# Moving the fourth weight sum's products later in three kinds of pair, its adding transfer into halves, one weight sum's transfer sooner, and one turned panel's reads to GpSimd's queue, in a two-layer encoder kernel

## The chip, the cores and the metric

The kernel runs on one core of a Trainium2 chip. The metric is device time in microseconds (us), the median of several runs. The profile is that of one execution on that core.

## The reference, cut to what matters

There are 256 tokens of width 2048, and two layers. Both layers end in the same kind of MLP, with a hidden width of 8192, and all matrices are float32:

```python
def sq_relu_mlp(h, g, w1, w2):
    a = jax.nn.relu(rms_norm(h, g) @ w1)
    return (a * a) @ w2
# layer 1:  proj = rms_norm(h) @ a_w_in -> q, k, v, forget gates
#           h = h + forgetting_attention(...) @ a_w_out
#           h = h + sq_relu_mlp(h, mlp_norm_g[0], mlp_w1[0], mlp_w2[0])
# shared:   kv = rms_norm(h) @ kv_w
# layer 2:  q = rms_norm(h) @ b_w_q ; chunked attention against kv
#           h = h + o @ b_w_out
#           h = h + sq_relu_mlp(h, mlp_norm_g[1], mlp_w1[1], mlp_w2[1])
```

The two MLPs are about 1270 us of the profiled span. The change touches them and the step ahead of each, the output projection of the attention.

## The kernel before, in words

**A unit of weights.** Weights come in units of 128 partitions x 1024 float32. ScalarE (ACT in the profile) rounds a unit to `hi` (line 323), and VectorE (DVE) makes `lo = raw - hi` (line 324). TensorE (PE) then multiplies in three passes: `hi` with the activations' `hi` (line 592), `hi` with the activations' `lo` (594), and `lo` with the activations' `hi` (596). So the second pass is the first that needs the activations' `lo`, and the third the first that needs the weights' `lo`. There are three buffers of `hi` and three of `lo`. A split can be issued when the unit three places earlier has been through its second pass.

**Pairs.** Two neighbouring panels of 512 output columns form a pair. For one half of the rows of a pair's weight matrix, the 2 x 2 blocks of tokens and columns go through seven products in place of eight, in the manner of Strassen and Winograd. The seven operands, or forms, are in this order 11, T3, T2, T1, 21, T4 and 22. The four T's are sums of weights:

- T3 = 22 + 12 and T2 = T3 + 11 are made by VectorE (`make`, line 964).
- T1 = 12 + 11 and T4 = T2 + 21 are made by a transfer that adds (`put`, line 974): GpSimd's queue sends the second operand from memory into the tile of the first.

Each form of the pairs here is two units (halves 0 and 1, six matmuls each). The other half of the rows goes the ordinary way, as units a4 to a7 (first panel) and b4 to b7 (second panel), of twelve matmuls each. b5, b6 and b7 of a pair are mixed into the start of the next pair.

**The order of pairs.** The hidden width is cut into four chunks c of 2048. W1(c,r) is the pair of the first matrix that gives hidden panels n = 2r and 2r+1 of chunk c, and W2(c,r) is the pair of the second matrix that uses chunk c. They run as W1(0,0), W1(0,1), then for each c: W2(c,0), W1(c+1,0), W2(c,1), W1(c+1,1). In the tables of the code W1(0,1) is called "second", W1(c,0) and W1(c,1) "ahead0" and "ahead1", and W2(c,0) and W2(c,1) "deep0" and "deep1".

**What sets the order.** `TABLES["ORD"]` gives for each kind of pair how the last three forms (F, named by `FO`) stand among the ordinary units. `run` goes through the units, and each time `fetch` sees to it that three splits are issued ahead. After each ordinary unit, and after each second half of a form, one call of `run_fill` issues one slot of side work. VectorE, ScalarE, TensorE and SyncE (SP, which issues most loads) keep the written order; GpSimd's order is the scheduler's.

**Side work.** A finished hidden panel is turned by 32 x 32 blocks (VectorE, line 440, tile z), crosses partitions by sixteen small transfers, half from SP's queue and half from GpSimd's (`hop`, line 466, into tile q), and then goes through `take`: relu in q (ACT line 1037), its square as `act` hi (ACT line 1042), the square in q (ACT line 1044), and `act` lo = q - hi (DVE line 1048). `TABLES["T"][n]` says, for chunks 1 to 3, in which slot after the panel's end each of these steps is issued. Panel 3 of chunk c ends with b7 of W1(c,1), inside W2(c,0), and the first unit that reads it is a6 of W2(c,0).

**Loads.** A pair's six numbers, such as `W2S`, say how many ordinary units before its start blocks 12, 22, 21 and 11 are loaded (SP's queue) and T3 and T1 are made, in this order. A load waits until the tile's old content has been split.

**The panel ahead of the MLP.** Each of the four finished panels of the residual stream is turned in the same way but through memory: one write, then four reads, both from SP's queue (`carry`, lines 450 and 456).

## Time and profile before

| what | value |
|---|---|
| device time, median of 3 runs | 2055.9 us (2054.76 to 2056.26) |
| span of the profiled execution, first to last instruction | 2051.8 us (no time of its own is given beside the span) |
| instructions | 27095 |
| PE busy | 2042.6 us, 9062 matmuls |
| DVE busy / ACT busy / POOL busy | 1784.1 / 1404.8 / 244.2 us |
| DMA | 557.78 MB, mean 272 GB/s |
| granted TensorE clock | 1.000 |

The span leaves 4.1 us of the median to what lies before the first and behind the last instruction. A busy PE is not by itself a PE at its peak, since matmuls overlap; whether it loses time is read from the starts of its matmuls and from its waits.

### The profile page before, as it was taken

The numbers are of one execution on the slowest core, as the hardware profiler recorded it, in microseconds if no ns is written. First come the engines' busy times: TensorE is split into PE (matmuls) and PEld (weight loads), VectorE is DVE, ScalarE is ACT, GpSimd is POOL, SyncE is SP. The second block draws the span as 40 slices with busy tenths as digits, with TensorE's granted clock in tenths as the row PEclk, the third lists the DMA queues.
The fourth block names the chain that finished last, engine by engine and source line by source line (L and its number), as shares of the span: only waits on it lengthen the run. The fifth ranks groups of instructions, "written<-read, shape, count | busy, mean of one in ns | idle before, by whom it ended". The sixth has DMA issues, their size and how long they took to land.

```text
span 2051.8 us, 27095 instructions
## 1 busy us (share of the span) xinstructions
PE 2042.6 (100%) x9062; PEld 1688.9 (82%) x9062; DVE 1784.1 (87%) x2065; ACT 1404.8 (68%) x1805; POOL 244.2 (12%) x351
## 2 busy tenths in 40 slices
PE   9999999999999999999999999999999999999999
PEld 8888888878888888888878888888888888888887
DVE  7788798899898898899988788889988988988996
ACT  7766676677677676677778666667866676776764
POOL 1121010021111102101012111100111111111020
PEclk9999999999999999999999999999999999999999
DMA  8898888898888898898879888888988888988985
GB/s 321 259 293 273 272 279 245 306 268 266 296 258 285 259 297 271 248 292 273 264 242 300 278 256 285 258 264 286 286 290 267 271 262 289 264 287 261 295 260 149
DMA packets 175021, 557.78 MB, mean 272 GB/s; under 512 B 40592, under 2 KB 69152, under 8 KB 152096
## 3 DMA queue, kind: packets, MB, share of 16 engines
q1 hardware_dynamic: 153824, 464.99, 63.7%
q0 software_dynamic: 20768, 90.75, 22.5%
q8 instruction: 71, 1.16, 0.2%
q14 instruction: 70, 0.57, 0.1%
q10 hardware_dynamic: 288, 0.30, 0.1%
HBM read 516.07 MB, written 27.29 MB: 265 GB/s over the span
## 4 chain that ended last, share of the span: by engine, by line
PE 94%; DVE 3%; DMA 1%; ACT 1%; issue 1%; SPq 0%; ACTq 0%; POOL 0%; DVEq 0%; POOLq 0%
PE acc L596 22%; PE acc L592 22%; PE acc L594 22%; PE s L596 9%; PE s L592 9%; PE s L594 9%; DVE lo L324 1%; DMA raw<-in_w_in 1%; PE po L729 1%; PE po L766 1%; ACT hi L323 0%; PE po L767 0%; PE po L728 0%; DMA turn<-z 0%; DMA raw<-in_w_qb 0%
## 5 line engine op out<-in xcount | busy, mean ns | idle before, releaser
L324 DVE TENSOR_TENSOR lo<-raw,hi 128x1024 fp32r<-128x1024 f32 (+1 forms) x409 | 494.1, 1212 | 80.4 <-ACT hi L323 76.3
L323 ACT ACTIVATE hi<-raw 128x1024 fp32r<-128x1024 f32 (+1 forms) x409 | 429.7, 1054 | 192.2 <-PE acc L594 131.0
L592 PE MATMUL acc<-hi,act 128*128 128x512 f32 x1774 | 496.2, 392 | 1.2 <-ACT hi L323 1.1
L596 PE MATMUL acc<-lo,act 128*128 128x512 f32 x1774 | 491.1, 390 | 1.5 <-DVE lo L324 1.4
L594 PE MATMUL acc<-hi,act 128*128 128x512 f32 x1774 | 490.3, 389 | 0.0
L596 PEld LDWEIGHTS acc<-lo,act 128*128 128x128 f32 x1774 | 332.3, 188 | 73.2 <-DVE lo L324 4.2
L594 PEld LDWEIGHTS acc<-hi,act 128*128 128x128 f32 x1774 | 332.9, 188 | 69.7
L592 PEld LDWEIGHTS acc<-hi,act 128*128 128x128 f32 x1774 | 331.4, 188 | 69.8 <-ACT hi L323 1.9
L323 ACT ACTIVATE hi<-w 128x1024 fp32r<-128x1024 f32 x254 | 267.1, 1058 | 127.9 <-PE acc L594 85.2
L324 DVE TENSOR_TENSOR lo<-wT,hi 128x1024 fp32r<-128x1024 f32 x220 | 267.1, 1221 | 65.0 <-ACT hi L323 61.4
L324 DVE TENSOR_TENSOR lo<-w,hi 128x1024 fp32r<-128x1024 f32 x254 | 305.5, 1218 | 15.3 <-ACT hi L323 13.5
L323 ACT ACTIVATE hi<-wT 128x1024 fp32r<-128x1024 f32 x220 | 232.0, 1060 | 97.3 <-PE acc L594 46.2
L592 PE MATMUL s<-hi,act 128*128 128x512 f32 x530 | 146.3, 391 | 0.2 <-ACT hi L323 0.2
L596 PE MATMUL s<-lo,act 128*128 128x512 f32 x530 | 145.2, 389 | 0.4 <-DVE lo L324 0.3
L594 PE MATMUL s<-hi,act 128*128 128x512 f32 x530 | 144.8, 388 | 0.0
L466 POOL DMA_DIRECT2D q<-z x192 | 95.6, 511 | 251.8 <-DVE z L440 217.3
L596 PEld LDWEIGHTS s<-lo,act 128*128 128x128 f32 x530 | 99.0, 188 | 22.0 <-DVE lo L324 1.7
L594 PEld LDWEIGHTS s<-hi,act 128*128 128x128 f32 x530 | 99.3, 188 | 20.7
L592 PEld LDWEIGHTS s<-hi,act 128*128 128x128 f32 x530 | 98.9, 188 | 20.9 <-ACT hi L323 0.8
L596 PE MATMUL s<-lo,S 128*128 128x512 f32 x288 | 88.8, 389 | 0.7 <-DVE lo L324 0.7
L592 PE MATMUL s<-hi,S 128*128 128x512 f32 x288 | 89.4, 392 | 0.0
L594 PE MATMUL s<-hi,S 128*128 128x512 f32 x288 | 88.7, 389 | 0.0
(217 smaller groups left out, 2285.6 us busy)
## 6 DMA issues: line engine op xcount, KB each, us to landing
raw<-in_w_in SPq DMA_DIRECT2D x75, 512.0 KB, 5.8
w<-in_w2fa SPq DMA_DIRECT2D x32, 1024.0 KB, 6.5
w<-in_w2fb SPq DMA_DIRECT2D x32, 1024.0 KB, 6.0
w<-in_w1fa SPq DMA_DIRECT2D x28, 1024.0 KB, 6.9
w<-in_w1fb SPq DMA_DIRECT2D x28, 1024.0 KB, 7.6
raw<-in_w2sa SPq DMA_DIRECT2D x52, 512.0 KB, 7.4
raw<-in_w2sb SPq DMA_DIRECT2D x50, 512.0 KB, 6.8
raw<-in_w_kv SPq DMA_DIRECT2D x48, 512.0 KB, 5.1
```

The costliest lines, as they stand in the source:

```text
L323: S.activation(hi[:, c], raw[:, c], AF.Copy)
L324: V.tensor_tensor(lo[:, c], raw[:, c], hi[:, c].bitcast(F32), op=ALU.subtract)
L466: (G if i % 2 else SY).dma_start(dst[32 * j : 32 * j + 32, i * n : (i + 1) * n], z[32 * i : 32 * i + 32, j * n : (j + 1) * n])
L592: TE.matmul(ps[:, cols], xh, cut(hi, j), start=first, stop=False, **kw)
L594: TE.matmul(ps[:, cols], xl, cut(hi, j), start=False, stop=False, **kw)
L596: TE.matmul(ps[:, cols], xh, cut(lo, j), start=False, stop=last, **kw)
L729: TE.matmul(s[:, P : 3 * P], q[:, a, P:T], k[:, a], start=True, stop=True)
L766: TE.matmul(po[:, :T], v[:, 0, a * P : (a + 1) * P], pT[:, :2], start=True, stop=False)
```

## The change

It has five parts.

1. In the pairs W2(c,0) with c of 1 to 3 (new kind "later0") T4 moves behind b4; in W1(c,0) and W1(c,1) with c of 1 to 3, T4 moves behind a5. The products are the same.
2. In all pairs of this kind (`deep`) the transfer that adds 21 into T2 is issued in two halves, each as soon as its half of T2 has been split. Before, only W1(0,1) did so.
3. In the pairs W2(c,1) the transfer that makes T1 is issued two ordinary units before the pair's start, not one.
4. For hidden panel 3 of chunks 1 to 3, the four steps of `take` are issued in slots 5, 6, 6, 6 after the panel's end, not in 4, 5, 5, 5.
5. The four reads of the last turned residual panel ahead of each MLP go to GpSimd's queue.

```diff
-    "FO": {..., "deep1": "456", "deep0": "465"},
+    "FO": {..., "deep1": "456", "deep0": "465", "later0": "465"},
-    "ORD": {..., "ahead1": "a4 F F a5 a6 a7 F b4", "ahead0": "F a4 F a5 a6 a7 F b4", ...
+    "ORD": {..., "ahead1": "a4 F a5 F a6 a7 F b4", "ahead0": "F a4 a5 F a6 a7 F b4", ...
         "deep0": "a4 F F F b4 a5 a6 a7",
+        "later0": "a4 F F b4 F a5 a6 a7"},
-    "T": (..., (0, -1, 4, 5, 5, 5)),
+    "T": (..., (0, -1, 5, 6, 6, 6)),
-    "W2L": (6, 5, 5, 5, 3, 1),
-    "W2S": (7, 7, 4, 5, 3, 1),
+    "W2L": (6, 5, 5, 5, 3, 2),
+    "W2S": (7, 7, 4, 5, 3, 2),
...
-                add(None, w2f, w2s, i, WIDE2, "deep%d" % q, ...
+                add(None, w2f, w2s, i, WIDE2, "later0" if c and not q else "deep%d" % q, ...
...
-        elif form and form.pair.order == "second" and form.name == "T2":
+        elif form and form.pair.deep and form.name == "T2":
             put(form.pair, "T4", int(half))
...
-            way.extend(i[0] for i in carry(*zt, 0, G if kept is not None and n == NG - 1 else SY)[:2])
+            way.extend(i[0] for i in carry(*zt, 0, G if n == NG - 1 else SY)[:2])
```

One line is added to the tables, so that a line after it has a number higher by one in the changed kernel.

**ScalarE in W2(1,0) of the first layer.** `w_5427` is block 22 of this pair, wT its T4; the raw and zraw that follow are its units b4, a5, a6 and a7, and the next w belongs to the next pair. Before:

```order
L323 ACTIVATE hi<-w_5427 128x1024 x2
L323 ACTIVATE hi<-wT_5499 128x1024 x2
L323 ACTIVATE hi<-raw 128x1024
L323 ACTIVATE hi<-zraw 128x1024
L1037 ACTIVATE q<-q 128x1024
L323 ACTIVATE hi<-raw 128x1024
L1042 ACTIVATE act<-q 128x1024
L1044 ACTIVATE q<-q 128x1024
L323 ACTIVATE hi<-raw 128x1024
```

With the change (block 22 is now `w_5431`):

```order
L324 ACTIVATE hi<-w_5431 128x1024 x2
L324 ACTIVATE hi<-raw 128x1024
L324 ACTIVATE hi<-wT_5479 128x1024 x2
L324 ACTIVATE hi<-zraw 128x1024
L324 ACTIVATE hi<-raw 128x1024
L1038 ACTIVATE q<-q 128x1024
L324 ACTIVATE hi<-raw 128x1024
L1043 ACTIVATE act<-q 128x1024
L1045 ACTIVATE q<-q 128x1024
```

Unit b4 now stands ahead of T4. The relu stands behind the split of a6 instead of that of a5, and the two squares behind the split of a7 instead of that of a6.

**VectorE at the same place.** Line 964 is the sum T3 of the next pair. Before:

```order
L324 TENSOR_TENSOR lo<-wT_5499,hi 128x1024 x2
L324 TENSOR_TENSOR lo<-raw,hi 128x1024
L324 TENSOR_TENSOR lo<-zraw,hi 128x1024
L324 TENSOR_TENSOR lo<-raw,hi 128x1024
L1048 TENSOR_TENSOR act<-q,act 128x1024
L964 TENSOR_TENSOR wT_5882<-w_5791,w_5687 128x1024
L324 TENSOR_TENSOR lo<-raw,hi 128x1024
```

With the change:

```order
L325 TENSOR_TENSOR lo<-raw,hi 128x1024
L325 TENSOR_TENSOR lo<-wT_5479,hi 128x1024 x2
L965 TENSOR_TENSOR wT_5858<-w_5796,w_5692 128x1024
L325 TENSOR_TENSOR lo<-zraw,hi 128x1024
L325 TENSOR_TENSOR lo<-raw,hi 128x1024 x2
L1049 TENSOR_TENSOR act<-q,act 128x1024
```

The last step of `take` now follows the split of a7, where it followed that of a6. The first half of the next pair's sum moves ahead of the split of a5.

**GpSimd's queue from W2(0,0) to W2(0,1) of the first layer.** w is a T1, wT a T4, and q<-z the small transfers of a hidden panel. Before:

```order
L974 DMA wT_4145<-in_w2fa 128x2048
L466 DMA q<-z 32x256 x8
L974 DMA w_4330<-in_w1fa 128x2048
L974 DMA wT_4527<-in_w1fa 128x2048
L466 DMA q<-z 32x256 x8
L974 DMA w_4671<-in_w2fa 128x2048
L974 DMA wT_4838<-in_w2fa 128x2048
```

With the change:

```order
L975 DMA wT_4145<-in_w2fa 128x1024 x2
L467 DMA q<-z 32x256 x8
L975 DMA w_4331<-in_w1fa 128x2048
L975 DMA wT_4528<-in_w1fa 128x1024 x2
L467 DMA q<-z 32x256 x3
L975 DMA w_4673<-in_w2fa 128x2048
L467 DMA q<-z 32x256 x5
L975 DMA wT_4840<-in_w2fa 128x1024 x2
```

T4's transfer is in two pieces, and T1 of W2(0,1) stands in the middle of the eight small transfers of hidden panel 0, where it stood behind them.

## The prediction, made before the result

> **What bounds the kernel now.** I read the page's busy times and its chain first, then TensorE's waits and the busy time by stretch in the MLPs.

> ```profile
> PE 2042.6 (100%) x9062; PEld 1688.9 (82%) x9062; DVE 1784.1 (87%) x2065; ACT 1404.8 (68%) x1805; POOL 244.2 (12%) x351
> PE 94%; DVE 3%; DMA 1%; ACT 1%; issue 1%; SPq 0%; ACTq 0%; POOL 0%; DVEq 0%; POOLq 0%
> ```

> TensorE is busy all through and makes 94% of the chain. A stretch inside the first layer's MLP says whether it is also at its pace. Columns: stretch and its length, then busy time and count for PE, weight loads, DVE, ACT and POOL, granted clock, DMA share and GB/s. The second block is TensorE's waits from 420 us on, the third the place of the longest.

> ```profile
> 475.00:1020.00 545.00, 545.00 (x2405) 451.21 (x2405) 490.62 (x484) 376.26 (x400) 59.62 (x100) 1.00 0.88 274
> ...
> PE acc L596 <- DVE lo L324: 1.7, 2, 1.4
> PE s L596 <- DVE lo L324: 0.7, 1, 0.7
> ...
> 433.80 0.72 PE L596 MATMUL acc<-lo,act 128*128 128x512 f32 x2 [1.35 <-DVE lo L324]
> ```

> From 475 to 1020 us 2405 matmuls fill 545.00 us, 0.2266 us each, with no wait. So the MLPs run at TensorE's pace, but for 2.4 us of waits. This caps a gain: if all of those 2.4 us went, the span would be 0.12% shorter. 0.2% of the time is 4.1 us, about what a measurement of this kernel tells from no change. A loss has no such cap: whatever delays TensorE inside a pair is paid in full, and four parts of the change apply in every chunk.

> **Part 4, with W2(c,0) of part 1: the late steps of panel 3.** This is the term that I expect to decide. In W2(1,0) of the first layer the rows before are these (TensorE, then ScalarE, then VectorE; the last two are the same place in the last chunk of the second layer):

> ```profile
> 642.12 0.62 PE L592 MATMUL acc<-hi,act 128*128 128x512 f32 x2
> 643.48 0.62 PE L592 MATMUL acc<-hi,act 128*128 128x512 f32 x2
> 644.84 1.07 PE L592 MATMUL acc<-hi,act 128*128 128x512 f32 x4
> 647.56 1.07 PE L592 MATMUL acc<-hi,act 128*128 128x512 f32 x4
> 650.28 1.07 PE L592 MATMUL acc<-hi,act 128*128 128x512 f32 x4
> 651.19 1.07 PE L594 MATMUL acc<-hi,act 128*128 128x512 f32 x4
> ...
> 643.23 1.06 ACT L323 ACTIVATE hi<-zraw 128x1024 fp32r<-128x1024 f32 x1 [0.30 <-PE acc L594]
> 644.19 1.04 ACT L1037 ACTIVATE q<-q 128x1024 f32<-128x1024 f32 x1
> 645.14 1.04 ACT L323 ACTIVATE hi<-raw 128x1024 fp32r<-128x1024 f32 x1
> 646.09 1.04 ACT L1042 ACTIVATE act<-q 128x1024 fp32r<-128x1024 f32 x1
> 647.16 1.06 ACT L1044 ACTIVATE q<-q 128x1024 f32<-128x1024 f32 x1
> ...
> 648.26 1.23 DVE L1048 TENSOR_TENSOR act<-q,act 128x1024 fp32r<-128x1024 f32 x1 [0.82 <-ACT q L1044]
> ...
> 1994.24 1.07 PE L594 MATMUL acc<-hi,act 128*128 128x512 f32 x4
> ...
> 1991.31 1.23 DVE L1048 TENSOR_TENSOR act<-q,act 128x1024 fp32r<-128x1024 f32 x1 [0.81 <-ACT q L1044]
> ```

> TensorE's rows are T4's halves (642.12, 643.48), b4 (644.84), a5 (647.56) and a6 (650.28). The second pass of a6, at 651.19, is the first work that needs `act` lo of panel 3. VectorE has it at 648.26 + 1.23 = 649.49, so 1.70 us are spare. At the sixth such place (three chunks in two layers) it is 1994.24 - 1992.54 = 1.70 again.

> Now the same times with the new order, TensorE at its pace: b4 at 642.12, T4's halves at 644.84 and 646.20, a5 at 647.56 and a6 at 650.28 as before. A split is released 1.11 us after the start of the six-matmul unit three places earlier: the split of a5 starts at 643.23, T4's first half at 642.12. So:

> - the split of a6 (three behind T4's first half) starts at 644.84 + 1.11 = 645.95;
> - relu follows 0.96 later (643.23 to 644.19), 646.91;
> - the split of a7 0.95 later (644.19 to 645.14), 647.86; T4's second half would allow 647.31;
> - the square into `act` 0.95 later (645.14 to 646.09), 648.81; the square in q 1.07 later (646.09 to 647.16), 649.88;
> - `act` lo 1.10 later (647.16 to 648.26), 650.98, and it ends at 652.21.

> TensorE wants it at 651.19, so its second pass waits 1.02 us. The first pass of a6 needs only the first square, done at 648.81 + 1.04 = 649.85, and is on time. Six places give 6 x 1.02 = 6.1 us. Nothing gives this back, since TensorE is the bound; the splits behind it only gain lead.

> The bounds: if ScalarE reached the squares one slot ahead of this reckoning (2.72 us, the length of a5 from 647.56 to 650.28), the price would be nil. If one more row of VectorE (1.23 us) came between, it would be 2.25 us, or 13.5 in all. I take 1.0, since it follows row by row from spacings at this very place.

> **The sum T3 in VectorE's way.** At this place T3's first half now stands ahead of the split of a5, and needs block 22, which SP issues after its small transfers.

> ```profile
> 638.93 0.99 SPq L936 DMA_DIRECT2D w<-in_w1fa  x2
> ...
> w<-in_w1fa SPq DMA_DIRECT2D x28, 1024.0 KB, 6.9
> ```

> It lands at about 638.93 + 6.9 = 645.8, and the sum ends at 647.1. Splits of a5 and a6 follow by 649.4, that of a7 by 650.6 or so, still ahead of 650.98. So I add nothing; a landing 1 us later would add up to as much to the stall.

> **T4 later and in halves.** What this can win is ScalarE's wait for T4 in the steady stretch (475 to 1020 us), and what covers it is the lead of the splits.

> ```profile
> ACT hi L323 <- DMA wT<-in_w1fa: 6.1, 4, 2.6
> ...
> wT<-in_w2fa POOLq DMA_DIRECT2D x8, 1024.0 KB, 10.5
> wT<-in_w1fa POOLq DMA_DIRECT2D x2, 512.0 KB, 10.8
> ```

> Those four waits, 6.1 us, stand in the very stretch in which TensorE never waits. So they cost nothing now, and their going gains nothing. Moving T4 by one unit gives its transfer 2.72 us more, and the first half starts one split earlier. The 28 added issues fall on GpSimd, which is busy 12% of the time: nothing.

> The two rows of half size (W1(0,1), the one pair in halves before) land no sooner than whole ones, 10.8 against 10.5 us. [...]

> **T1 sooner, amid the small transfers.** For W2(c,1) T1 now stands behind three of the eight pieces of panel 0 on GpSimd's queue. Rows before (POOL without, then with a T1 ahead; then the relu that waits for the pieces, and b7, the unit behind it):

> ```profile
> 529.22 3.97 POOL L466 DMA_DIRECT2D q<-z  x8 [23.75 <-DVE z L440]
> ...
> 608.41 0.86 POOL L974 DMA_DIRECT2D w<-in_w2fa  x1 [20.95 <-DVE wT L964]
> 610.84 3.49 POOL L466 DMA_DIRECT2D q<-z  x7 [1.56 <-DVE z L440]
> 616.97 0.50 POOL L466 DMA_DIRECT2D q<-z  x1 [2.64 <-DMA w<-in_w2fa]
> ...
> w<-in_w2fa POOLq DMA_DIRECT2D x8, 1024.0 KB, 9.4
> DMA to landing us min/median/max: 2.8/5.5/6.4
> ...
> 543.73 1.05 ACT L1037 ACTIVATE q<-q 128x1024 f32<-128x1024 f32 x1
> 544.68 1.04 ACT L323 ACTIVATE hi<-raw 128x1024 fp32r<-128x1024 f32 x1
> 546.90 1.07 PE L592 MATMUL s<-hi,act 128*128 128x512 f32 x4
> ```

> With a T1 ahead, the eighth piece was not issued until T1 had landed, and none came in before it: 610.84 + 6.4 = 617.2 the first, 616.97 + 2.8 = 619.8 the last, that is 8.8 to 11.4 us after T1's issue. In the new order T1 follows three pieces of 0.5 us, near 530.8, and lands near 540.2 by the median; the pieces behind it come at 539.6 to 542.2, or a little later. The relu wants them at 543.73, and the split behind it (ends 545.72) has 1.2 us to spare. So nothing, with a bound of some 1 us at six places if the queue is slower.

> SP's load of 21 for these pairs now, and the two loads of ordinary units that it moves ahead of (one's split, and its kind):

> ```profile
> 526.78 0.33 SPq L936 DMA_DIRECT2D w<-in_w2fa  x1
> 538.03 1.06 ACT L323 ACTIVATE hi<-zraw 128x1024 fp32r<-128x1024 f32 x1 [1.21 <-PE s L594]
> zraw<-in_w1sa SPq DMA_DIRECT2D x12, 512.0 KB, 8.3
> ```

> That load of 21 waits there until 526.8 as now. The two loads behind it then start at 526.78 + 0.33 = 527.1 and land near 527.1 + 8.3 = 535.4; they are wanted at 538.03 and later, so 2.6 us cover this.

> **The residual panel's reads.** ScalarE's rows where the last turned panel arrives, and the unit behind it:

> ```profile
> 397.01 0.91 ACT L417 ACTIVATE y<-q,gsb 128x256 f32<-128x256 f32 x2 [2.00 <-DMA q<-turn]
> 397.82 1.04 ACT L323 ACTIVATE hi<-raw 128x1024 fp32r<-128x1024 f32 x1
> 402.82 1.07 PE L592 MATMUL acc<-hi,act 128*128 128x512 f32 x4
> ```

> ScalarE waits 2.0 us for them now, but the split behind them, of W1(0,0)'s a6, is issued 5.0 us ahead of a6 itself (397.82 and 402.82). Whether GpSimd's queue brings them 2 us sooner or later, TensorE does not see it: nothing.

> The wait at 433.80 has none of this in its way: W1(0,1) keeps its order.

> **Sum.** The span goes from 2051.8 to about 2057.9 us, and with the 4.1 us around it the median from 2055.9 to 2062.0.

> **Rivals.** (a) Faster: the transfers move out of the way of the few waits, the one at 433.80 above all. For it: that wait stands where the first hidden panel's steps pass, which hang on transfers. Against it: all rows there keep their order. All 2.4 us would give 2053.5, and it needs the stall of part 4 to be absent.
> (b) No change: side work at a6 comes earlier than I reckon, so that panel 3 is in time. It decides from a shift of 1.0 us. For it: if T4's splits start without a wait, ScalarE has a lead it does not have now. Against: the release rule, which ties a6's split to T4's first half. Time 2055 to 2058 (up to 0.3 us at each place).
> (c) Slower still: panel 0's pieces land late behind T1, or block 22 late for T3. Another 0.3 to 1 us at six places gives 2064 to 2068.

> **How the numbers follow.** My forecast, 0.8 to 1.3 us at six places (2060.5 to 2064), has 0.66; (c) 0.13; (b) 0.17, (a) 0.04, of which hardly anything passes 0.2%. So slower 0.79, same 0.19, faster 0.02. The range leaves out (a), most of (b) and the end of (c): 2057.5 to 2067, which also holds the 1.5 us by which the runs before differ.

> **What would show it.** TensorE's waits should list the second pass of a6 waiting for VectorE's `act` (line 1049) six times, near 0.9 us each (a pass lasts 1.07 us and the next starts after 0.91, so 0.16 of the 1.02 does not count as idle). ScalarE's waits for T4 should shrink. If those six waits are absent, the prediction is wrong by its main term; if GpSimd's pieces or block 22 hold ScalarE or VectorE, by (c).

## The result: 14.4 us slower, in three places of which the forecast had one

| | before | with the change |
|---|---|---|
| device time, median of 5 runs | 2055.82 us (2054.47 to 2056.26) | 2070.24 us (2067.41 to 2073.25) |
| ratio to before, 95% interval | 1 | 1.0071 (1.0059 to 1.0083) |
| span of the profiled execution | 2051.8 us | 2071.0 us (its own time 2072.82 us) |
| PE busy / POOL busy | 2042.6 / 244.2 us | 2049.6 / 276.2 us |

The forecast was 2062.0 with a range of 2057.5 to 2067.0: the right direction, and less than half of the size. In all five runs of the changed kernel the time is 1.8 us above the span, so the 4.1 us between the span and the median of before were not all work around the span; the profiled execution of before was a quick one, that of the changed kernel near the slowest of its five, 2.6 us above the median.

From the profile of the changed kernel: the stretch that answers to 475 to 1020 us (length, then busy time and count of PE, weight loads, DVE, ACT and POOL, granted clock, DMA share, GB/s), and TensorE's waits from 395 us on (total, times, longest).

```profile
480.00:1025.00 545.00, 541.22 (x2378) 445.50 (x2377) 484.34 (x476) 371.70 (x394) 71.51 (x112) 1.00 0.88 272
...
PE acc L595 <- DVE act L1049: 5.5, 6, 0.9
PE acc L593 <- ACT act L421: 4.1, 2, 2.5
PE acc L597 <- DVE lo L325: 1.7, 2, 1.4
PE s L597 <- DVE lo L325: 1.1, 1, 1.1
PE s L593 <- ACT hi L324: 0.9, 1, 0.9
```

In 545 us TensorE now does 2378 matmuls where it did 2405. The first row of waits is the forecast one: six waits of 0.91 us for `act` lo. The second and the last are new and were not in the sum. To size them in TensorE's own time I laid the starts of its 9062 matmuls, one by one, beside those of before; the table has what each place adds.

| place | forecast | from the two traces | back alone gives | alone costs |
|---|---|---|---|---|
| a6 of W2(c,0), six places (parts 1 and 4) | 6.1 | 7.3 | 6.0 or 5.3 | 7.1 |
| a6 of W1(0,0), two places (part 5) | 0 | 4.7 + 2.3 | 4.2 | 5.3 |
| b7 of W1(c+1,0), at the start of W2(c,1), six places (parts 1 and 3) | 0 | 3.7 | 4.3 or 4.0 | 3.7 |
| sum, us | 6.1 | 17.9 | 14.5 | 16.1 |

The last two columns are differences of medians from the experiments below; each is uncertain by some 2 to 3 us. The sums are near the measured 14.4; that from the traces is larger, as 19.2 us lie between the spans of the two profiled executions. In the recorded expectations below these shares stand as 6.9, 6.9 and 4.0 us.

**The place that was forecast.** W2(1,0) of the first layer, TensorE, ScalarE, then VectorE:

```profile
651.29 0.61 PE L593 MATMUL acc<-hi,act 128*128 128x512 f32 x2
...
656.73 1.07 PE L593 MATMUL acc<-hi,act 128*128 128x512 f32 x4
658.70 1.20 PE L595 MATMUL acc<-hi,act 128*128 128x512 f32 x4 [0.91 <-DVE act L1049]
...
652.39 1.07 ACT L324 ACTIVATE hi<-raw 128x1024 fp32r<-128x1024 f32 x1 [0.75 <-PE acc L595]
653.36 1.04 ACT L1038 ACTIVATE q<-q 128x1024 f32<-128x1024 f32 x1
654.31 1.04 ACT L324 ACTIVATE hi<-raw 128x1024 fp32r<-128x1024 f32 x1
655.26 1.04 ACT L1043 ACTIVATE act<-q 128x1024 fp32r<-128x1024 f32 x1
656.33 1.06 ACT L1045 ACTIVATE q<-q 128x1024 f32<-128x1024 f32 x1
...
651.25 1.23 DVE L965 TENSOR_TENSOR wT<-w,w 128x1024 f32<-128x1024 f32 x1 [0.61 <-DMA w<-in_w1fa]
657.42 1.23 DVE L1049 TENSOR_TENSOR act<-q,act 128x1024 fp32r<-128x1024 f32 x1 [0.81 <-DMA zraw<-in_w2sa]
```

T4's first half starts at 651.29, which was 644.84 in the reckoning, so 6.45 us lie between the two clocks. With them the reckoned chain is 652.40, 653.36, 654.31, 655.26, 656.33 and 657.43; the rows have it to 0.01 us. Without a wait the second pass would start 0.91 after a6, at 657.64; it starts 1.06 later (1.02 forecast).

**The turned residual panel.** First layer, W1(0,0). First row: before, the product that makes `act` hi of the last panel. The others are of the changed kernel: ScalarE's rows there, TensorE's last pass of a5 and the three of a6, and the busy times from 407 to 411 us, with the granted clock (0.57) behind the five engines.

```profile
399.70 1.06 ACT L420 ACTIVATE act<-y 128x1024 fp32r<-128x1024 f32 x1
...
402.22 0.91 ACT L418 ACTIVATE y<-q,gsb 128x256 f32<-128x256 f32 x2 [6.67 <-DMA q<-turn]
404.90 1.06 ACT L421 ACTIVATE act<-y 128x1024 fp32r<-128x1024 f32 x1
...
402.44 1.07 PE L597 MATMUL acc<-lo,act 128*128 128x512 f32 x4
406.01 1.19 PE L593 MATMUL acc<-hi,act 128*128 128x512 f32 x4 [2.50 <-ACT act L421]
407.27 2.08 PE L595 MATMUL acc<-hi,act 128*128 128x512 f32 x4
409.14 1.77 PE L597 MATMUL acc<-lo,act 128*128 128x512 f32 x4
...
407.00:411.00 4.00, 3.93 (x11) 2.97 (x11) 3.96 (x5) 1.91 (x2) 0.00 (x0) 0.57 0.50 167
```

ScalarE waits 6.67 us for the reads, where it waited 2.00. What a6 needs is `act` hi of that very panel, ready at 399.70 + 1.06 = 400.76 before, 2.06 us ahead of a6's 402.82. Now it is ready at 405.96, and TensorE waits 2.50 us. Then it pays a second time: the granted clock falls to 0.57 over 4 us, and the next two passes take 1.87 and 1.61 us in place of 0.91 each, 1.7 us more.

**Panel 0's small transfers.** The changed kernel, from W2(0,0) to W2(0,1) of the first layer: SP's issues, GpSimd's, the landing times of SP's and then of GpSimd's eight pieces, and the relu; behind the last dots the same two landing rows of before.

```profile
531.74 0.33 SPq L937 DMA_DIRECT2D w<-in_w2fa  x1
532.11 0.43 SPq L300 DMA_DIRECT2D zraw<-in_w1sa  x1
532.59 0.43 SPq L300 DMA_DIRECT2D raw<-in_w1sa  x1
533.12 0.67 SPq L300 DMA_DIRECT2D raw<-in_w2sa  x1
533.90 9.40 SPq L467 DMA_DIRECT2D q<-z  x8
...
534.17 1.54 POOL L467 DMA_DIRECT2D q<-z  x3 [23.74 <-DVE z L441]
535.70 0.97 POOL L975 DMA_DIRECT2D w<-in_w2fa  x1
536.30 2.38 POOL L467 DMA_DIRECT2D q<-z  x4
540.45 0.51 POOL L467 DMA_DIRECT2D q<-z  x1 [1.76 <-DMA q<-z]
...
DMA to landing us min/median/max: 7.6/12.6/13.3
DMA to landing us min/median/max: 5.9/10.6/12.3
...
550.81 1.06 ACT L1038 ACTIVATE q<-q 128x1024 f32<-128x1024 f32 x1 [2.02 <-DMA q<-z]
...
DMA to landing us min/median/max: 3.3/4.5/4.9
DMA to landing us min/median/max: 3.8/4.2/4.7
```

Not only the five pieces behind T1 are late, but all eight on SP's queue, where T1 does not stand. There the load of 21 (531.74) is followed by two loads of ordinary units and then by a third, 1.5 MB in all, directly ahead of the pieces. Before, only the third (527.20) stood between the two.

### The profile page after: what moved, and what is told of

Same layout as the page of the kernel before. It is cut to its first block, busy times and chain, and to the rows that moved or that the text cites. A ratio compares the mean times of both kernels' runs of the same rounds, so it can differ in the third digit from the quotient of the medians.

```text
span 2071.0 us, 27141 instructions
## 1 busy us (share of the span) xinstructions
PE 2049.6 (99%) x9062; PEld 1687.7 (81%) x9062; DVE 1785.0 (86%) x2065; ACT 1405.1 (68%) x1805; POOL 276.2 (13%) x387
## 3 DMA queue, kind: packets, MB, share of 16 engines
q8 instruction: 71, 1.16, 0.2%
## 4 chain that ended last, share of the span: by engine, by line
PE 70%; DMA 5%; DVE 3%; ACT 2%; issue 1%; SPq 0%; ACTq 0%; POOL 0%; DVEq 0%; POOLq 0%
PE acc L595 16%; PE acc L597 16%; PE acc L593 16%; PE s L593 7%; PE s L597 7%; PE s L595 7%; DVE lo L325 2%; DMA raw<-in_w2sa 1%; ACT hi L324 1%; DMA wT<-in_w1fb 1%; DMA q<-z 1%; DMA raw<-in_w1b 1%; DMA q<-turn 0%; DVE act L1049 0%; DMA zraw<-in_w2sa 0%
## 5 line engine op out<-in xcount | busy, mean ns | idle before, releaser
L324 ACT ACTIVATE hi<-raw 128x1024 fp32r<-128x1024 f32 (+1 forms) x409 | 429.6, 1054 | 214.8 <-PE acc L595 150.3
L324 ACT ACTIVATE hi<-w 128x1024 fp32r<-128x1024 f32 x254 | 266.6, 1057 | 106.6 <-PE acc L595 67.3
L324 ACT ACTIVATE hi<-wT 128x1024 fp32r<-128x1024 f32 x220 | 233.1, 1061 | 96.3 <-PE acc L595 56.7
## 6 DMA issues: line engine op xcount, KB each, us to landing
raw<-in_w_in SPq DMA_DIRECT2D x75, 512.0 KB, 5.7
w<-in_w2fa SPq DMA_DIRECT2D x32, 1024.0 KB, 6.5
w<-in_w2fb SPq DMA_DIRECT2D x32, 1024.0 KB, 6.7
w<-in_w1fa SPq DMA_DIRECT2D x28, 1024.0 KB, 7.3
w<-in_w1fb SPq DMA_DIRECT2D x28, 1024.0 KB, 6.9
raw<-in_w2sa SPq DMA_DIRECT2D x52, 512.0 KB, 8.6
raw<-in_w2sb SPq DMA_DIRECT2D x50, 512.0 KB, 7.7
raw<-in_w_kv SPq DMA_DIRECT2D x48, 512.0 KB, 5.4
```

The source lines that it names most:

```text
L324: S.activation(hi[:, c], raw[:, c], AF.Copy)
```

## The experiments

**Each part taken back.** Four kernels, each the changed one but for one edit.

Part 5 back:

```diff
-            way.extend(... G if n == NG - 1 else SY)[:2])
+            way.extend(... G if kept is not None and n == NG - 1 else SY)[:2])
```

> The changed kernel with part 5 undone: the four reads of the last turned residual panel go back to SP's queue. Theory (the parts add up): in the trace after, TensorE's starts fall behind those of before by 4.7 us at unit a6 of W1(0,0) in the first layer (0.54 to 5.22) and by 2.2 us in the second (11.04 to 13.20), so 6.9 us go and the time is near 2070.2 - 6.9 = 2063.3. Rival (the reads are late because the half transfers and the later T4 load the queues and engines, not because of the queue that they stand on): the reads stay late by 3 to 5 us and the time stays near 2070.

Measured 2066.06 us, 1.0049 (1.0036 to 1.0062): 4.2 us of the forecast 6.9. a6 of the second layer no longer waits; that of the first still waited 0.8 us (not the 1.6 us of an expectation below) and lost 1.5 us of TensorE's starts, its reads having landed 8.3 to 9.3 us after their issue from SP's queue too (5.7 to 5.9 before). So landings scatter in this stretch from run to run, and part of the 4.7 us of the trace was that.

Part 3 back (`"W2S": (7, 7, 4, 5, 3, 1)`, `"W2L": (6, 5, 5, 5, 3, 1)`):

> The changed kernel with part 3 undone: T1 of the pairs W2(c,1) goes out one ordinary unit before the pair again. Theory (the pieces of panel 0 on both queues are held up by T1's transfer): the relu waits for the pieces vanish (2.02, 1.02, 1.09 us and so on in the trace after), and with them the slips at the six places, 1.45 + 0.48 + 0.58 + 0.42 + 0.76 + 0.35 = 4.0 us: near 2066.2. Rival (the pieces are late for other reasons, since SP's own pieces, issued from 533.90 on, before T1 at 535.70, were late as well): the waits stay and the time stays near 2070.

Measured 2065.92 us, 1.0052 (1.0038 to 1.0066): the theory's value in time. But the relu waits did not vanish. Of 6.8 us at the six places in the changed kernel's trace 3.8 were left, and TensorE's starts still lost 1.8 us there, where they had lost 3.7. So T1 is not the whole cause; see below.

Part 4 back (`(0, -1, 4, 5, 5, 5)`):

> The changed kernel with part 4 undone: take of panel 3 in slots 4, 5, 5, 5 again, T4 still behind b4. Theory (the slots make the wait): the relu stands behind the split of a5, that of a6 behind the relu; act lo ends near 650.4 on the clock of before where it is wanted at 651.19, so the six waits of a6 (0.91 us each, 1.15 us of TensorE's starts) vanish: 2070.2 - 6.9 = 2063.3. Rival (the order with T4 behind b4 alone is enough, since it releases the splits a unit later): the six waits stay, near 2070.

later0 back (`"deep%d" % q` for all):

> The changed kernel with later0 undone: W2(c,0) has T4 ahead of b4 again, take of panel 3 stays in slots 5, 6, 6, 6. By the same reckoning act lo then ends near 651.4 on the clock of before, 0.2 us late: the six waits shrink to some 0.2 us or less, and the time is near 2070.2 - 6.9 + 1.2 = 2064.5. Rival (the slots alone make the whole wait): the six waits stay at 0.9 us, near 2070.

Measured 2064.20 us, 1.0039 (1.0027 to 1.0052), and 2064.92 us, 1.0047 (1.0033 to 1.0061). In both the six waits are gone from TensorE's list. The order alone (part 4 back) leaves 0.87 of the 1.70 us that panel 3 had to spare: `act` lo ends at 655.34 and the pass that needs it starts at 656.21. The slots alone (later0 back) use up all of it: `act` lo ends at 656.14, the pass starts at 656.20, 0.08 us late, and TensorE's starts lose 0.22 to 0.26 us at each of the six places, 1.4 us in all, about as reckoned. Only the two together make the wait of 0.91 us.

**The three together, and what is left.**

> The changed kernel with parts 3, 4 and 5 undone together; T4's later place in the three kinds of pair and its transfer in halves stay. Undone one at a time they gave 4.2, 4.3 and 6.0 us, together 14.5 us of the 14.4 that the change costs. Theory (parts 1 and 2 cost nothing, the three add up): 2055.8, within 1 us of before, and the six waits of a6 absent. Rival (SP's load of block 21, which part 1 moves ahead of two loads of ordinary units, still puts 1 MB in front of the pieces of panel 0, or the undone parts overlap): 2058 to 2061, with relu waits for the pieces left in W1(c+1,0).

Measured 2054.95 us, 0.9997 (0.9988 to 1.0006): as before. The later T4 of W1(c,0) and W1(c,1), its halves and later0 cost nothing by themselves that the time shows, nor do they gain. The profile shows a small cost: the relu waits for panel 0 at three of the six places, 2.6 us in all, and TensorE's starts lose 1.4 us.

**Each suspect alone, on the kernel before.**

```diff
 # e6: part 5 alone
+            way.extend(... G if n == NG - 1 else SY)[:2])
 # e8: part 3 alone
+    "W2L": (6, 5, 5, 5, 3, 2),
+    "W2S": (7, 7, 4, 5, 3, 2),
 # e10: the same reads on ScalarE's queue
+            way.extend(... G if kept is not None and n == NG - 1 else S if n == NG - 1 else SY)[:2])
```

> The kernel before with part 5 alone: the last turned residual panel is read on GpSimd's queue. Theory (the part costs by itself what undoing it gave back): 2055.9 + 4.2 = 2060.1, with TensorE waiting for ScalarE's product of this panel (line 420) at a6 of W1(0,0) in both layers. Rival (most of the lateness is the scatter of landings in that stretch, since with part 5 undone a6 of the first layer still waited 1.6 us): within 2 us of 2055.9.

Measured 2060.90 us, 1.0024 (1.0014 to 1.0035): 5.3 us, the theory.

> The kernel before, with the reads of the last turned residual panel on ScalarE's queue instead of SP's. Theory (the reads are late because SP's next loads no longer stand behind them and share the transfer engines with them): they land 8 to 10 us after issue as from GpSimd's queue (5.8 from SP's before), and the time is near 2060. Rival (GpSimd's queue itself makes them late): they land within 6 to 7 us and the time stays within 2 us of 2055.9. ScalarE issues in order, so up to 2 us of its own idle time there go into the issues.

Measured 2065.97 us, 1.0051 (1.0038 to 1.0063), worse than from GpSimd's queue. Landing times of the four reads in the first layer: before (SP), with part 5 alone (GpSimd), on ScalarE's queue, and last from a kernel in which SP's queue holds 1 MB less ahead of them (below):

```profile
DMA to landing us min/median/max: 5.7/5.8/5.9
...
DMA to landing us min/median/max: 6.9/8.6/9.4
...
DMA to landing us min/median/max: 7.4/10.9/12.9
...
DMA to landing us min/median/max: 3.5/3.7/4.0
```

These four are single traces, and landings scatter. Over all the traces, both layers, with the loads ahead unchanged, the median landing is 5.8 to 9.1 us on SP's queue, 7.8 to 9.9 on GpSimd's and 10.1 to 10.9 on ScalarE's. What TensorE's starts lose at a6 in the two layers together separates more clearly: 0 to 2.1 us in the seven traces with the reads on SP's queue, 3.4 to 7.0 in the six on GpSimd's, 11.0 on ScalarE's.

So the change of queue is the cause, and it is not GpSimd's queue as such. Why is argued, not shown: on SP's queue the reads stand ahead of SP's next loads (before, they go out from 389.24 us on and the next load at 391.60), and on any other they share the 16 transfer engines with these (with the reads on ScalarE's queue, 94.3% of the engines' time from 389 to 394 us went to SP's queue and 1.6% to ScalarE's). The one trace with a load taken from ahead of them (3.7 us) and the one on ScalarE's queue fit this; that another trace on SP's queue had 9.1 us says that the queue is not all. The loss on ScalarE's queue is seen at a6: its last read lands in the first layer 6.5 us later than before on TensorE's clock, TensorE waits 4.22 and 2.87 us, and each time the granted clock falls to half behind the wait (409.77 to 413.19 us and 1433.77 to 1437.18 us).

> The kernel before with part 3 alone: T1 of W2(c,1) goes out two ordinary units before the pair. Here SP's load of 21 keeps its place, so only T1's transfer (1 MB) gets ahead of panel 0's last five pieces of GpSimd's queue. Theory (T1's transfer alone makes the relu late): 2055.9 + 4.3 = 2060.2, relu waits of 1 to 2 us at the six places. Rival (it takes the load of 21 and the two loads behind it, moved by part 1, as well): panel 0 is in time as I forecast, no wait above 0.5 us, 2055 to 2057.

Measured 2056.05 us, 1.0003 (0.9994 to 1.0012): the rival. T1 sooner, by itself, costs nothing that can be measured, and the relu waits at none of the six places. GpSimd's last piece lands at 543.35, and this kernel's clock is 1.16 us behind (its first piece goes out at 530.38, that of before at 529.22): 542.2, the end of the window in the prediction.

**The two halves of one cause.** Part 3 with the new order of W1(c,0), on the kernel before; and the changed kernel with block 21 loaded one unit later:

```diff
 # e12
+    "W2L": (6, 5, 5, 5, 3, 2),
+    "W2S": (7, 7, 4, 5, 3, 2),
+    "ORD": {..., "ahead0": "F a4 a5 F a6 a7 F b4", ...
 # e13
-    "W2L": (6, 5, 5, 5, 3, 2),
-    "W2S": (7, 7, 4, 5, 3, 2),
+    "W2L": (6, 5, 4, 5, 3, 2),
+    "W2S": (7, 7, 3, 5, 3, 2),
```

> The kernel before with part 3 and the new order of W1(c,0) alone. By itself neither cost anything (T1 alone 2056.1 with the last piece of panel 0 landing at 543.35 in its trace; the orders and halves alone 2055.0 with the last piece at 541.4; 536.8 before; the relu wants them near 543.7). Theory (the two use up the same cover of 6.9 us: T1 stands ahead of five pieces, and block 21's load, moved ahead of two loads of ordinary units, puts these 1 MB right ahead of the pieces of SP's queue): together they make the relu late by 1 to 2 us at six places, 2055.6 + 4.3 = 2060. Rival (it takes the halves or the later T4 of W2(c,0) too): within 1.5 us of before.

> The changed kernel with block 21 of the pairs W2(c,1) loaded one ordinary unit later (the third number of W2S 3, that of W2L 4), so that SP's two loads of ordinary units go out ahead of it again; T1 stays sooner. Theory (the place of block 21's load is the other half of the cause): the relu waits for panel 0's pieces go, 2070.2 - 4.3 = 2066. Rival (T1's transfer against the new order of the units is what matters, whatever SP does): 2070, relu waits as in the changed kernel.

Measured 2059.60 us, 1.0018 (1.0009 to 1.0027), and 2066.26 us, 1.0051 (1.0038 to 1.0063). Landing times of panel 0's pieces, SP's and then GpSimd's, with T1 alone, with the orders and halves alone (the three parts back), and with T1 and the order of W1(c,0); then the relu that waits for the pieces, at the first of the six places: in the last kernel, in the changed one with part 3 back, and in the changed one with 21 later:

```profile
DMA to landing us min/median/max: 4.7/5.5/8.1
DMA to landing us min/median/max: 4.4/8.3/9.5
...
DMA to landing us min/median/max: 5.0/8.1/8.5
DMA to landing us min/median/max: 6.2/6.6/6.9
...
DMA to landing us min/median/max: 7.6/12.1/13.0
DMA to landing us min/median/max: 6.1/10.0/11.8
...
545.05 1.06 ACT L1037 ACTIVATE q<-q 128x1024 f32<-128x1024 f32 x1 [1.26 <-DMA q<-z]
...
546.56 1.06 ACT L1038 ACTIVATE q<-q 128x1024 f32<-128x1024 f32 x1 [1.01 <-DMA w<-in_w2fa]
...
545.85 1.05 ACT L1038 ACTIVATE q<-q 128x1024 f32<-128x1024 f32 x1
```

Before, the last piece landed at 536.8 and the relu came at 543.73, 6.9 us later. T1 alone takes 5.4 of these us (542.2), the order alone 5.1 (its last piece lands at 541.4, on a clock 0.5 us ahead: 541.9). Here each fits; both do not. Taking either one back gives some 4 us.

The two halves are not equal, though. With T1 and the order of W1(c,0) the relu waits at all six places, 7.3 us in all. With the order but not T1 it still waits: at three places with the three parts back, at four with part 3 alone back, the first among them (the second row). With 21 later, or in the kernel before with T1 alone, it waits at none. So in the traces the place of block 21's load weighs more than T1 does.

**The main term by itself.** Part 4 and later0 on the kernel before:

> The kernel before with part 4 and the order later0 of W2(c,0) alone: the main term of the prediction by itself. Theory: six waits of a6's second pass for act lo (line 1049 in the changed kernel), 0.9 us each, TensorE's starts 1.1 to 1.2 us later at each, 2055.6 + 6.3 = 2062. Rival (the other parts load the queues and make panel 3 late as well): less than half of that, 2056 to 2058.

Measured 2062.99 us, 1.0037 (1.0024 to 1.0049): 7.1 us, against 6.1 in the prediction (7.3 by TensorE's starts in its trace), with the six waits word for word as in the changed kernel:

```profile
PE acc L595 <- DVE act L1049: 5.5, 6, 0.9
```

**A try at a faster kernel.**

```diff
-    "T0H": ((1, -1, 6, 6, 6, 6, 6, 8, 8), ...
+    "T0H": ((1, -1, 6, 6, 6, 6, 7, 8, 8), ...
-    "W1IH": (10, 7, 6, 8, 4, 2),
+    "W1IH": (10, 7, 6, 7, 4, 2),
```

> A try at a faster kernel: the one before, with two numbers changed. In W1(0,1) of the first layer the four small sums of hidden panel 0 (line 395 on) go one slot later, behind the split's lo for which TensorE waits 1.35 us at 433.80; and block 11 of that pair is loaded one ordinary unit later, behind the reads of the last turned residual panel, so that 1 MB less stands ahead of them on SP's queue. Theory: the first gives 1.35 us, the second lets the reads land some 2 us sooner, which takes away a wait at a6 of W1(0,0) that some profiles show (1.5 us with T1 alone changed) and the one of before does not: 2055.6 - 1.35 - 0.7 = 2053.5. Rival (the landings in that stretch scatter too much): 2055, no difference.

Measured 2055.78 us, 0.9997 (0.9988 to 1.0005): the rival. The reads did land after 3.7 us, and the wait at 433.80 did go, but a wait came back one half unit on, longer:

```profile
435.15 0.72 PE L596 MATMUL acc<-lo,act 128*128 128x512 f32 x2 [1.54 <-DVE lo L324]
```

No version ran that beats the kernel before.

## Why the prediction was partly right, point by point

The one term that the sum held was right. Two terms that it put at nothing were not: panel 0's pieces (3.7 to 4.3 us) and the residual panel's reads (4.2 to 5.3 us).

- **Part 4 with later0** ("the term that I expect to decide"): right. The chain came out as reckoned, and the part alone cost 7.1 us. The reckoning took 1.02 us at each place; beside the 1.06 us of the late pass the matmul behind a wait starts about 0.1 us late too (starts of the same matmuls: 1.20 to 1.25 us at each of the six places).
- **The sum T3**: right. Block 22 was there by 651.25, 1.0 us sooner than reckoned, and VectorE had caught up by the split of a7, ahead of which it stood idle for 0.64 us. So `act` lo was not delayed.
- **T4 later and in halves**: right. ScalarE's wait for T4 in the steady stretch went from 6.1 to 0.9 us, and the time did not follow: with this part in place and the three others back it was as before.
- **T1 amid the small transfers**: wrong in the sum, right for T1 alone. The step "the pieces behind it come at 539.6 to 542.2" held with T1 alone. In the changed kernel they came 3.3 us later (550.40 on a clock 4.95 us behind: 545.45). The step that failed is the next one, on SP's load of 21: I saw the two loads move behind it and asked only whether they themselves are in time ("2.6 us cover this"). They are. But they now stand directly ahead of panel 0's pieces, and so use the same 6.9 us as T1. Rival (c) had the place, with a bound of 1 us at six places and too small a chance.
- **The residual panel's reads**: wrong twice. The cover of 5.0 us was that of the weights' split behind the reads; TensorE's a6 waits sooner for `act` hi of the panel itself, made by the product at 399.70, with 2.06 us to spare, and these in a trace with quick reads: in three of the other traces with the reads on SP's queue a6 waited too. And "2 us sooner or later" was no bound: from GpSimd's queue the last read landed at 402.11, where it was 396.90; with 0.53 us between the clocks that is 4.7 later. On SP's queue the reads had gone out ahead of SP's next loads, and the sum did not count the loss of this place. The landings fit in the main: medians of 5.8 to 9.1 us where SP's next loads stand behind the reads, 7.8 to 10.9 where they run beside them. They overlap, so the place alone does not give the price.
- **The clock**: not in the forecast at all. A stall of 2.50 us cost 4.7, since the granted clock was 0.50 for 3.41 us behind it (407.20 to 410.61).

## What to carry to other kernels

A cover is spent once: when two edits each fit into the same slack, or nearly (6.9 us ahead of a relu, 1.70 us ahead of a second pass), reckon both against it together, and ask of every transfer that is moved what now stands behind it, not only whether it is itself in time. Do not take a move of a small urgent read to an idle queue for free: here both idle queues made it later (median landing in the first layer 8.6 and 10.9 us, where it was 5.8). To find the cover of a wait, follow the waiting data itself to its reader, not the next instruction on the engine.

## What the hardware showed that I had not expected

In these traces the granted clock fell after some short idle times of TensorE and not after others. Part 5 alone, first layer: a wait of 1.77 us, then the busy times of two stretches of 3.41 us (behind the five engines stands the granted clock). Then the same of the changed kernel with 21 later: a wait of 2.34 us.

```profile
405.82 1.57 PE L592 MATMUL acc<-hi,act 128*128 128x512 f32 x4 [1.77 <-ACT act L420]
403.04:406.45 3.41, 1.64 (x8) 1.04 (x7) 1.87 (x2) 3.38 (x5) 0.00 (x0) 1.00 1.01 399
406.45:409.86 3.41, 3.41 (x10) 2.42 (x9) 3.38 (x4) 1.88 (x3) 0.00 (x0) 0.50 0.52 198
...
404.55 1.21 PE L593 MATMUL acc<-hi,act 128*128 128x512 f32 x4 [2.34 <-ACT act L421]
400.05:403.46 3.41, 2.15 (x10) 1.46 (x8) 0.82 (x1) 2.68 (x6) 0.00 (x0) 1.00 1.02 418
403.46:406.87 3.41, 2.27 (x9) 1.56 (x10) 2.72 (x3) 2.94 (x3) 0.00 (x0) 1.00 0.97 378
```

Take the steps of 3.41 us between these points, from 10 us on. In those that ended at one of the four falls inside a kernel TensorE was idle for 1.77, 2.22, 2.67 and 2.87 us; in those that no fall followed, for 1.65 us at most. So 1.77 us of a step was enough here and 1.65 us was not, and each fall lasted one step. The wait of 2.34 us lay astride a boundary, 403.46, and its two steps were idle for 1.26 and 1.14 us, as the rows show (3.41 less TensorE's busy time). So in these executions it went by where the boundaries fell (406.45, 406.87 and 407.20 us in the traces with part 5 alone, with 21 later and of the changed kernel) whether such a wait was paid twice.
